# The left operands of a Strassen-like matmul kernel are placed at 32 different offsets in their ring tiles

## The chip, the cores and the metric

The kernel runs on one core of one Trainium2 chip, as one launch. The metric is device time in microseconds (us), from the first to the last instruction of the launch. Engines are named as in the profile: PE is the matmul engine, PEld its weight load, DVE the vector engine, ACT the activation engine, POOL the general-purpose engine, SP the engine that issues most DMAs. A matmul here has a left operand (128 columns, loaded into the array as weights, PEld) and a right operand (up to 512 columns, streamed through it).

## The reference

One decoder block on 1024 tokens of width 1024, in float32:

```python
def reference(x, mem, norm_mix, w_in, ...):
    h = x
    for i in range(DEPTH):                      # DEPTH = 1
        h = h + hybrid_mixer(rmsnorm(h, norm_mix[i]), w_in[i], ...)
        h = h + mem_cross_attention(rmsnorm(h, norm_xattn[i]), rmsnorm(mem, norm_mem[i]), ...)
        h = h + swiglu(rmsnorm(h, norm_ffn[i]), w_ffn_in[i], w_ffn_out[i])
    return rmsnorm(h, norm_final)
```

The mixer multiplies the normed input by `w_in` (1024 x 7712), runs two recurrent branches (an SSD scan with 16 heads and a gated linear attention with 4 heads) on slices of the product, multiplies each by a 1024 x 1024 matrix, gates and adds them, and multiplies by `w_o`. Cross-attention has four heads on 256 memory tokens. The feed-forward layer (FFN) is `(silu(n @ w_g) * (n @ w_u)) @ w_ffn_out` with 2816 hidden columns.

## The kernel before

**Arithmetic.** Activations are held transposed: 128 channels in the partitions, tokens along the row. Every large product is computed as three matmuls in the type fp32r: each operand is split into a high part (ACT copies it with rounding to fp32r) and a low part (DVE subtracts the high part from the source), and high x high, high x low and low x high are summed in PSUM. `split` (L226) is that pair of instructions.

**Units.** The products with `w_in` and with the two input matrices of the FFN use a seven-product (Strassen-like) scheme. A `Unit` takes 256 columns of the weight matrix and 1024 of its rows, as a raw tile of 8 KB per partition. `Operands` holds the seven combinations of the right operand (`B11`, `B21`, `T1`, `B22`, `T2`, `T3`, `T4`), each split into a high and a low tile, once for all units. For each of the seven products, `Unit.step` forms the left combination from the raw tile (some of these need an addition on DVE or POOL, into a tile named `sa`), takes one high and one low tile from a ring (`wring`, L230; names `whi` and `wlo`, three buffers of each, 640 fp32 wide), splits into them, and issues 12 matmuls: four blocks of 128 columns (`k`), three matmuls each, into one PSUM bank. `evac` then adds the bank into the unit's output, on DVE or ACT. The left operand of block `k` is `hi[:, k*128:(k+1)*128]`, that is 512 bytes per partition.

There are 48 units: 26 for `w_in`, made in the order conv inputs (6), `z` (4), `r` (4), `q` and `k` (4), the two gates (4 and 4), and 22 for the FFN, made later (a gate unit and an up unit for each of 11 column blocks). So 48 x 7 x 12 = 4032 matmuls read their left operand from the ring.

**Other users of the ring.** The memory's key and value products (`kv_unit`, L574) and the product that gives `v` (`v_steps`, L675) take ring tiles as well, and so does a prefetch of gates (`gate`, L1338). In `v_steps` the ring tile is the right operand: 264 columns per block, so its blocks start 0 and 1056 bytes into the tile.

**Other large products.** `dense` (names `hl`, `wd`) and the second FFN matrix (names `fs`) take their operands from other tiles ("slots" of 8 KB).

**Where tiles lie.** A ring tile is 640 x 4 = 2560 bytes per partition, which is 5 x 512, and a slot is 8192 bytes, 16 x 512. In the built program the ring tiles and all slots that hold operands of fp32r matmuls begin at 128 modulo 512, so in a unit the left operand lies a multiple of 512 bytes from the right one.

**Order.** The instruction order on each engine is made by the framework's scheduler from the program order and priorities; the splits and the evacuations of a unit are issued with a raised priority (`ahead`, 200 steps). In the SSD stage PE's order is the program's own.

Of the kernel before, what the change touches and what calls it, by code (L numbers as in the profile page):

```python
# [10 lines left out]
F32R = mybir.dt.float32r  # L11
# [5 lines left out]
P = 128  # L17
# [61 lines left out]
def block_kernel(ctx: ExitStack, tc: tile.TileContext, t: dict, out: bass.AP):  # L79
# [10 lines left out]
    def pool(name, bufs=1, space=None, stack=None):  # L90
        kw = {"reuse_waits": "tile"} if space is None else {"space": space}
        return (stack or ctx).enter_context(tc.tile_pool(name=name, bufs=bufs, **kw))
# [3 lines left out]
    wp = pool("w", 3)  # L96
# [25 lines left out]
    def acc():  # L122
        return ps.tile([P, 512], F32, name="acc", tag="acc", bufs=4)
# [56 lines left out]
    gcol, at = {}, 0  # L180
# [45 lines left out]
    def split(src, hi, lo, e=None):  # L226
        ACT.activation(hi, src, AF.Copy)  # L227
        sub(e or DVE, lo, src, hi)

    def wring():  # L230

        return [wp.tile([P, 640], F32R, name=n, tag=n, bufs=3)[:, :528] for n in ("whi", "wlo")]

    class Operands:

# [13 lines left out]
        def __init__(s, hb, kh, first=None, key="op", swap=0, last_key=None, order=None):  # L249
            s.B, s.kh, s.key, s.done, s.swap = {}, kh, key, 0, swap  # L250
            s.order = order or tuple(s.PLAN)
            s.last_key = last_key or key
            s.steps = s.build(hb, kh, first or (lambda *a: None))
# [25 lines left out]
    class Unit:  # L279
# [6 lines left out]
        def __init__(s, W, row0, c0, kh=4, post=None, key="aux", okey=None, side=None):  # L286
            s.W, s.row0, s.c0, s.kh, s.post, s.key, s.okey, s.side = W, row0, c0, kh, post, key, okey or key, side or key
            s.raw = s.S1 = s.S2 = s.e = None

        def load(s):  # L290
            if s.raw is None:
                s.raw = slot(s.key, (P, 2 * s.kh, 256), name="raw")
                SP.dma_start(s.raw, s.W[s.row0:s.row0 + 256 * s.kh, s.c0:s.c0 + 256].rearrange("(k p) c -> p k c", p=P))
# [30 lines left out]
        def step(s, name, B, cs=ALL, again=False):  # L324
            s.load()
            kh = s.kh
            if name == "B11":
                s.banks, s.swap, s.u = {}, B.swap, False
                s.out()
            if again:  # L330
                wh, wl = s.w
            else:
                with ahead():
                    src = s.left(name)
                    hi, lo = wring()
                    s.w = wh, wl = [x[:, :kh * P].rearrange("p (k c) -> p k c", c=P) for x in (hi, lo)]
                    split(src, wh, wl)
            xh, xl = B[name]
            key = s.BANK[name]
            fresh = key not in s.banks  # L340
            if fresh:
                s.banks[key] = acc()
            p = s.banks[key]
            m = 0
            for k in range(kh):
                for x, y in ((wh, xh), (wh, xl), (wl, xh)):
                    PE.matmul(p[:, cs], x[:, k, :], y[:, k, cs], start=fresh and m == 0, stop=m == 3 * kh - 1,
                              skip_group_check=True)
                    m += 1
            s.evac(name, p, cs)  # L350
# [213 lines left out]
    def kv_unit(c0):  # L564
# [7 lines left out]
        for kk in range(4):  # L572
            with ahead():
                hi, lo = wring()  # L574
                hv = hi[:, :512].rearrange("p (k c) -> p k c", c=256)
                lv = lo[:, :512].rearrange("p (k c) -> p k c", c=256)
                split(raw[:, 2 * kk:2 * kk + 2, :], hv, lv)
            for i in range(2):
                o = pa[i][:, :256]
                for k2 in range(2):  # L580
                    k = 2 * kk + k2
                    for m, (x, y) in enumerate(((hv, mh), (lv, mh), (hv, ml))):
                        w_, m_ = x[:, k2, :], y[:, k, :]
                        if c0 < D:
                            PE.matmul(o, w_[:, i * P:(i + 1) * P], m_, start=k == 0 and m == 0, stop=k == 7 and m == 2)
                        else:
                            PE.matmul(o, m_[:, i * P:(i + 1) * P], w_, start=k == 0 and m == 0, stop=k == 7 and m == 2)
            yield
# [60 lines left out]
    def v_steps():  # L649
        for pr in range(2):  # L650
# [12 lines left out]
            for n, name in enumerate(CHAIN):  # L663
                parts = []
                with ahead():
                    if name == "T1":
                        add(DVE, sa, A21, A22)
                    elif name == "B22":
                        sub(DVE, sa, sa, A11)
                        sub(DVE, A12, A12, sa)  # L670
                    elif name == "T2":
                        sub(DVE, A21, A11, A21)
                    a = (A11, A12, sa, A12, sa, A21, A22)[n]
                    for k2 in range(2):
                        hi, lo = wring()  # L675
                        hv, lv = hi.rearrange("p (k c) -> p k c", c=HW), lo.rearrange("p (k c) -> p k c", c=HW)
                        split(a[:, 2 * k2:2 * k2 + 2, :], hv, lv)
                        parts.append((hv, lv))
# [791 lines left out]
    at = [Att(h, j) for h in range(4) for j in (1, 0)]  # L1470
# [16 lines left out]


    rbc2 = u_xo_stats.sum
    gu = []  # L1490
    for u in range(D_FF // 256):
        def gpost(i, j, ap):
# [194 lines left out]
    for x, (n, k, kn) in enumerate(todo):  # L1687
        name = CHAIN[n]
# [62 lines left out]
```

## Time and profile before

| what | value |
|---|---|
| median of 2 timed runs | 1947.66 us (1947.66 to 1947.67) |
| span of the profiled execution | 1949.0 us |
| PE busy | 1916.2 us, 9776 instructions |
| PEld busy | 1615.6 us |
| DVE busy | 1298.5 us |
| ACT busy | 845.8 us |
| POOL busy | 557.8 us |
| mean granted TensorE clock | 0.998 |

The profiled execution took 1949.0 us from its first to its last instruction, 1.3 us more than the median of the timed runs. A matmul's record lasts longer than the distance from its start to the next one's, because matmuls overlap in the array and their ends are modelled: what a matmul costs is read from the distance between starts, or from the length of a piece of the chain of waits divided by the matmuls in it. The mean duration in the table of groups is not that cost.

### The profile page before, as it was taken

To read this page: it belongs to the slowest core of one execution; us is meant where nothing else is said; L and a number is where in the kernel's file an instruction comes from. 1 tells how busy PE (TensorE), PEld (TensorE's weight loads), DVE (VectorE), ACT (ScalarE), POOL (GpSimd) and SP (SyncE) were. 2 spreads that over 40 slices of the span, in tenths; PEclk is the share of its full clock that TensorE was granted. 3 is DMA by queue.
4 is the path that set the end of the run, shared out by engine and by line. 5 is a ranking of instruction groups with operands and counts; after the bars stand their busy time and mean duration, and the time that the engine had idled before them with its cause. 6 is when DMAs were issued, how large, how long until landed. Compare 5 with 4: busy or idle time off the path is not lost.

```text
span 1949.0 us, 26264 instructions
## 1 busy us (share of the span) xinstructions
PE 1916.2 (98%) x9776; PEld 1615.6 (83%) x9776; DVE 1298.5 (67%) x1873; ACT 845.8 (43%) x1485; POOL 557.8 (29%) x428
## 2 busy tenths in 40 slices
PE   7999999999999999999999999999999999999998
PEld 7998787888878888788887888888888888888888
DVE  7766879877776764655534237677777777766566
ACT  7534564655553444643223235444333333345243
POOL 0012334345543231022433000006445544320002
PEclk9999999999999999999999999999999999999999
DMA  9423383446553653997675201442233224177463
GB/s 341 144 93 101 130 307 107 152 161 186 174 173 123 198 167 124 348 346 270 226 269 164 82 22 44 140 141 82 90 126 110 82 100 144 42 271 239 157 224 126
DMA packets 237875, 317.98 MB, mean 163 GB/s; under 512 B 16538, under 2 KB 156036, under 8 KB 237748
## 3 DMA queue, kind: packets, MB, share of 16 engines
q1 hardware_dynamic: 236020, 310.01, 47.4%
q10 hardware_dynamic: 1728, 6.29, 0.8%
q8 instruction: 77, 1.26, 0.3%
q14 instruction: 50, 0.41, 0.1%
HBM read 215.27 MB, written 100.99 MB: 162 GB/s over the span
## 4 chain that ended last, share of the span: by engine, by line
PE 43%; DMA 3%; POOL 2%; DVE 1%; issue 1%; ACT 1%; POOLq 0%; SPq 0%; DVEq 0%; ACTq 0%
PE acc L51 38%; PE bank L51 4%; DMA pre<-in_w_ffn_out_dram 1%; POOL pre L73 1%; DMA down_d<-pre 1%; PE bank L55 1%; POOL ssum L73 0%; DVE hl L73 0%; POOL sa L73 0%; DMA h_d<-ga 0%; DMA ga<-vm_d 0%; DVE wd L73 0%; ACT wd L227 0%; ACT sq L493 0%; DVE phl L73 0%
## 5 line engine op out<-in xcount | busy, mean ns | idle before, releaser
L51 PE MATMUL acc<-hl,wd 128*128 128x512 f32 x1920 | 440.4, 390 | 3.6 <-DVE wd L73 2.0
L51 PEld LDWEIGHTS acc<-hl,wd 128*128 128x128 f32 x1920 | 359.6, 188 | 80.7 <-DVE wd L73 3.3
L73 DVE TENSOR_TENSOR wlo<-raw,whi 128x512 fp32r<-128x512 f32 x272 | 236.4, 875 | 103.6 <-ACT whi L227 103.5
L227 ACT ACTIVATE whi<-raw 128x512 fp32r<-128x512 f32 x272 | 169.5, 629 | 247.6 <-PE acc L51 201.0
L73 DVE TENSOR_TENSOR o<-acc,o 128x512 f32<-128x512 f32 (+1 forms) x256 | 172.6, 676 | 108.8 <-PE acc L51 95.4
L51 PE MATMUL acc<-fs 128*128 128x512 f32 (+1 forms) x792 | 155.7, 356 | 0.1
L51 PEld LDWEIGHTS acc<-fs 128*128 128x128 f32 x792 | 130.7, 189 | 20.8 <-issue 0.5
L73 DVE TENSOR_TENSOR fs<-fr,fs 128x1024 fp32r<-128x1024 f32 (+1 forms) x84 | 98.9, 1217 | 36.5 <-ACT fs L227 36.4
L227 ACT ACTIVATE fs<-fr 128x1024 fp32r<-128x1024 f32 (+1 forms) x84 | 79.2, 982 | 95.9 <-PE acc L51 31.2
L73 POOL TENSOR_TENSOR raw<-raw,sa 128x512 f32<-128x512 f32 x44 | 57.1, 1297 | 207.8 <-DVE wlo L73 207.8
L73 POOL TENSOR_TENSOR sa<-raw 128x512 f32<-128x512 f32 x43 | 69.6, 1619 | 107.0 <-DMA raw<-in_w_in_dram 78.9
L227 ACT ACTIVATE whi<-sa 128x512 fp32r<-128x512 f32 x96 | 59.6, 626 | 93.7 <-PE acc L51 92.3
L73 DVE TENSOR_TENSOR wlo<-sa,whi 128x512 fp32r<-128x512 f32 x96 | 80.9, 843 | 13.7 <-ACT whi L227 12.7
L73 DVE TENSOR_TENSOR wd<-raw,wd 128x1024 fp32r<-128x1024 f32 x40 | 52.8, 1323 | 47.6 <-ACT wd L227 47.2
L73 POOL TENSOR_TENSOR rstd<-rstd,mhalf 128x4 f32<-128x4 f32 (+1 forms) x7 | 8.7, 1246 | 257.0 <-DVE rstd L73 257.0
L227 ACT ACTIVATE wd<-raw 128x1024 fp32r<-128x1024 f32 x40 | 42.2, 1057 | 90.4 <-PE acc L51 89.8
L51 PE MATMUL acc<-T4h,whi 128*128 128x512 f32 x192 | 76.3, 397 | 2.4 <-DVE o L73 2.4
L51 PE MATMUL acc<-B22h,wlo 128*128 128x512 f32 x192 | 75.7, 394 | 1.5 <-DVE wlo L73 1.5
L51 PE MATMUL acc<-T1h,whi 128*128 128x512 f32 x192 | 76.3, 397 | 0.0
L51 PE MATMUL acc<-T2h,whi 128*128 128x512 f32 x192 | 75.9, 395 | 0.0
L51 PE MATMUL acc<-T3h,whi 128*128 128x512 f32 x192 | 75.9, 395 | 0.0
L51 PE MATMUL acc<-B22h,whi 128*128 128x512 f32 x192 | 75.7, 394 | 0.0
(399 smaller groups left out, 4698.6 us busy)
## 6 DMA issues: line engine op xcount, KB each, us to landing
raw<-in_w_in_dram SPq DMA_DIRECT2D x26, 1024.0 KB, 5.9
raw<-in_w_ffn_in_dram SPq DMA_DIRECT2D x22, 1024.0 KB, 6.5
act_d<-o SPq DMA_DIRECT2D x77, 256.0 KB, 2.1
fr<-act_d SPq DMA_DIRECT2D x35, 512.0 KB, 7.9
pre<-in_w_ffn_out_dram SPq DMA_DIRECT2D x11, 1024.0 KB, 10.0
fr<-down_d SPq DMA_DIRECT2D x20, 512.0 KB, 3.9
down_d<-pre SPq DMA_DIRECT2D x33, 256.0 KB, 3.1
h_d<-ga SPq DMA_DIRECT2D x32, 256.0 KB, 3.1
```

The costliest lines, as they stand in the source:

```text
L51: return s.e.matmul(o, x, y, **kw)
L55: return s.e.transpose(o, x, i)
L73: return f(*a, **kw)
L227: ACT.activation(hi, src, AF.Copy)
```

## The change

A unit now gets a number when it is made (`place`), and keeps `at = 4 * (number % 32)` elements, that is 16 bytes times the number modulo 32. `wring(at)` returns the slice of each ring tile that starts there. The counter starts at 22 for the `w_in` units (offsets 352 to 496 bytes, then 0 to 240) and is set to 0 before the FFN's units (0 to 336 bytes). The tiles' size (640) and count are as before, so no other tile moves; the largest offset is 124 elements and a unit uses 512, which fits in 640. The other users of the ring call `wring()` and stay at offset 0. No instruction is added or taken away; the addresses that the splits write and the weight loads read are what changes.

```diff
-    def wring():
-
-        return [wp.tile([P, 640], F32R, name=n, tag=n, bufs=3)[:, :528] for n in ("whi", "wlo")]
+    place = [22]
+
+    def wring(at=0):
+
+        return [wp.tile([P, 640], F32R, name=n, tag=n, bufs=3)[:, at:min(at + 528, 640)] for n in ("whi", "wlo")]
...
             s.raw = s.S1 = s.S2 = s.e = None
+            s.at = 4 * (place[0] % 32)
+            place[0] += 1
...
-                    hi, lo = wring()
+                    hi, lo = wring(s.at)
...
     rbc2 = u_xo_stats.sum
+    place[0] = 0
     gu = []
```

## The prediction

> **What bounds the kernel now.** I read the page first: its span, the engines' busy time and the granted clock.
>
> ```profile
> span 1949.0 us, 26264 instructions
> PE 1916.2 (98%) x9776; PEld 1615.6 (83%) x9776; DVE 1298.5 (67%) x1873; ACT 845.8 (43%) x1485; POOL 557.8 (29%) x428
> PEclk9999999999999999999999999999999999999999
> ```
>
> PE is busy nearly all the time at full clock. Busy matmuls overlap, so I went on to the chain of waits in order of time, which gives a piece's length and its number of matmuls. Its columns are start, length, what.
>
> ```profile
> 1220.35 85.00 PE acc L51 x375
> ...
> 1320.48 459.26 PE acc L51 x2026
> 1779.74 59.84 PE bank L51 x264
> ```
>
> The first piece lies in the dense products (85.00 / 375 = 226.7 ns each), the second is nearly the whole first half of the FFN, where the left operands come from the ring (459.26 / 2026 = 226.7 ns), the third belongs to the second FFN matrix (59.84 / 264 = 226.7 ns). In all three one matmul follows another with no break: the kernel runs at PE's own rate, and what a 512-wide fp32r matmul costs from start to start is 226.7 ns in every one of them. The timeline inside the second piece shows the same from one matmul to the next (columns: start, length, then engine, line, operation):
>
> ```profile
> 1449.78 0.39 PE L51 MATMUL acc<-B22h,whi 128*128 128x512 f32 x1
> ...
> 1453.18 0.39 PE L51 MATMUL acc<-T4l,whi 128*128 128x512 f32 x1
> ```
>
> Fifteen steps lie between these two starts: 3.40 / 15 = 226.7 ns.
>
> **The change part by part.** The groups by line show whose operands move.
>
> ```profile
> L51 PE MATMUL acc<-hl,wd 128*128 128x512 f32 x1920 | 440.4, 390 | 3.6 <-DVE wd L73 2.0 <-ACT wd L227 1.4 <-DVE hl L73 0.2
> ...
> L51 PE MATMUL acc<-T4h,whi 128*128 128x512 f32 x192 | 76.3, 397 | 2.4 <-DVE o L73 2.4
> ...
> L51 PE MATMUL acc<-T4l,whi 128*128 128x512 f32 x192 | 74.7, 389 | 0.0
> ```
>
> The 21 groups from the second row to the third (the seven products by three) read the ring; 21 x 192 = 4032 matmuls, or 4032 x 226.7 ns = 914 us, 47% of the span. The groups on `hl,wd` and `fs` keep their addresses. Of the 48 units two get offset 0 (the first made for the FFN, and the eleventh of `w_in`, whose number is 32), so 46 x 84 = 3864 matmuls get a distance other than 0 modulo 512. One nanosecond on each is 3.9 us, 0.2%. Two per cent of 1947.66 us, about what a measurement of this kernel can tell from no change, is 39 us or 10.1 ns on each. That one number decides the case.
>
> *The weight load.* It reads the same 512 bytes per block, from another start.
>
> ```profile
> L51 PEld LDWEIGHTS acc<-B11h,wlo x192: 187/188/192, 161.5 to 1703.0; 128*128 128x128 f32 x192
> ```
>
> It takes 188 ns under a matmul step of 226.7, so it has 39 ns of cover. If it grew by less, nothing should show; if that cover goes, the excess is paid on each of the 3864.
>
> *The matmul, with its operands at another distance.* No fp32r unit matmul of this kernel has it, so this is the unknown cost, to be bounded by the nearest rows. The nearest are the `v` products: there the ring tile is the right operand, and of its two blocks one lies 0 and one 1056 bytes, 32 modulo 512, from the left one.
>
> ```profile
> 127.75 0.28 PE L51 MATMUL acc<-whi,B21h 128*128 128x264 f32 x1
> ...
> 128.12 0.28 PE L51 MATMUL acc<-whi,B21h 128*128 128x264 f32 x1
> ...
> 128.48 0.28 PE L51 MATMUL acc<-whi,B21h 128*128 128x264 f32 x1
> ```
>
> In the program's order the three matmuls from the first row on read the block at 0 and the three from the second row the block at 32: 0.37 us against 0.36. With the starts rounded to 0.01 us, three matmuls at 32 bytes take 0.01 us less, give or take 0.02, so each costs between 10 ns less and 3 ns more than at 0. The next nearest are transposes in plain fp32, whose operands are `ident` and a source: in the built program the source `xt` lies at 0 from it and the source `xz` at 128 one way, 384 the other, modulo 512.
>
> ```profile
> 18.73 1.47 PE L55 MATMUL bank<-ident,xt 128*128 128x128 f32 x12
> ...
> 439.76 0.60 PE L55 MATMUL bank<-ident,xz 128*128 128x128 f32 x4
> ```
>
> One record lasts 0.27 us in the groups, so the steps are (1.47 - 0.27) / 11 = 0.109 us and (0.60 - 0.27) / 3 = 0.110 us. Again no difference, with a full weight load under each step. The single-transpose duration behind it:
>
> ```profile
> L55 PE MATMUL bank<-ident,xt 128*128 128x128 f32 x64 | 8.3, 272 | 0.0
> ```
>
> I take 0 ns as the value, from the `v` rows, because those are fp32r matmuls with the same kind of weight load. They cover one distance of 31 and the transposes another in another type, so the ends of the range stay wide; what could be at the other distances is priced under the rivals.
>
> *The splits.* ACT and DVE write the ring from another start. The rows are of the view by tile (minimum, median and maximum in ns), of a window (busy us of PE, PEld, DVE, ACT and POOL, then the clock and the DMA) and of PE's waits (total us, times, longest).
>
> ```profile
> L73 DVE TENSOR_TENSOR wlo<-raw,whi x272: 658/685/1789, 9.8 to 1713.8; 128x512 fp32r<-128x512 f32 x136
> L73 DVE SCALAR_TENSOR_TENSOR cv<-o,cols,cv x36: 1273/1279/2303, 264.5 to 372.3; 128x1021 f32<-128x1021 f32 x12, 128x1022 f32<-128x1022 f32 x12, 128x1023 f32<-128x1023 f32 x12
> 1400.00:1600.00 200.00, 200.00 (x884) 165.63 (x883) 153.54 (x190) 67.37 (x116) 96.13 (x64) 1.00 0.30 99
> PE acc L51 <- DVE wlo L73: 3.7, 7, 1.7
> ```
>
> The convolution's writes start 12, 8 and 4 bytes into a row, and the three forms together run from 1273 to a median of 1279 ns, so a shifted write costs DVE nothing that shows; I take 0. Were it not so: in the FFN's stage DVE is busy 153.5 us of 200 and ACT 67.4 while PE has no break, and in the whole kernel PE waits 3.7 us for `wlo` in the matmuls into `acc`. A tenth more on a 685 ns split is 0.07 us in the 2.72 us of a product's 12 matmuls, under that cover. With the cover gone, 336 splits of 0.07 us would be 23 us.
>
> *The rest.* No instruction, DMA, wait or tile size is changed, and the ring keeps three buffers, so no queue is reordered by the diff itself.
>
> The sum against the profiled execution is 1949.0 + 0 = 1949.0 us. That span is 1.3 us over the median of the timed runs, 1947.66, so the forecast for a timed run is 1948.
>
> **The rivals.** *Slower: left and right reads get in each other's way at other distances.* The mechanism would sit in every unit matmul, where the next block's weights are read while the right operand streams. A price: the 256-wide matmuls of the last product give the part of a step that doesn't grow with the width.
>
> ```profile
> 1927.70 3.96 PE acc L51 x33
> ```
>
> A 256-wide step is 3.96 / 33 = 120 ns; two of them less one 512-wide step leave 240 - 226.7 = 13.3 ns of fixed cost. If a clash doubled it, 3864 x 13.3 ns = 51 us would be added: 1999 us; at half of the distances, 1973. It is over 2% from 10.1 ns on each. For it: all large matmuls of this kernel run at one distance, 0, so the trace hardly says what the others cost. Against it: the `v` rows and the transposes.
>
> *Faster: the fixed cost is itself a clash at distance 0, and goes.* [...]
>
> ```profile
> 704.85 0.60 PE L51 MATMUL bank<-v,attm 128*128 128x256 f32 x2
> 705.29 0.59 PE L51 MATMUL bank<-sm,qk 128*128 128x256 f32 x2
> 705.72 0.59 PE L51 MATMUL bank<-v,attm 128*128 128x256 f32 x2
> ```
>
> Each step there is 0.87 / 4 = 217.5 ns, 9.2 under 226.7. If the shifted distances brought the unit matmuls down to that, 3864 x 9.2 ns = 36 us would go: 1912 us; if the whole 13.3 ns went, 1896. Against it: those fp32 operands also lie at 0 modulo 512, so the lower cost there needs no other distance, and the `v` rows keep their cost at 32.
>
> [...]
>
> *The change doesn't reach the time*, because another wait hides it in either direction. In the FFN's piece PE has no break, so this could only be in part; its time is the forecast's.
>
> **How the numbers follow.** The forecast has 0.57 (1943 to 1953 is its own range), and the last rival 0.03 at the same time. The slower rival has 0.30, as the trace has little to say on 30 of the 31 distances; I give 0.24 of it to more than 2% and 0.06 to less, since a clash at few distances or of few ns stays under. The faster one has 0.10, half of it over 2%, which needs more than the fp32 rows' 9.2 ns. So faster 0.05, within 2% 0.71, slower 0.24. The range goes up to 1999, the doubled fixed cost, leaving out about a tenth above it, and down to 1930, half of the faster rival's 36 us, leaving out less than a tenth.
>
> **What would show it.** If I am right, the long piece of the chain in the FFN still gives 226.7 ns a matmul, in each unit, and PEld stays at 188 ns. If the slower rival is right, the steps differ from unit to unit with the unit's offset while `hl,wd` and `fs` stay at 226.7. If the faster one is, they fall toward 217 in most units and not in the FFN's first. If the splits are to blame, PE's waits for `wlo` grow, DVE's 685 ns rises, and the steps inside a product stay.

## The result and the profile after

The changed kernel took 1962.1 us (median of 2 runs, 1960.4 to 1963.8) against 1947.7 us before: ratio 1.0075, 95% interval 1.0056 to 1.0094. It is 0.75% slower, about 14.5 us, inside the 2% that was called no change and clear of the measurement's own scatter. The profiled execution is the run timed at 1963.8 us; that its span, 1962.1 us, equals the median is a coincidence.

The page of the changed kernel:

```profile
span 1962.1 us, 26264 instructions
PE 1932.2 (98%) x9776; PEld 1615.1 (82%) x9776; DVE 1299.9 (66%) x1873; ACT 848.2 (43%) x1485; POOL 555.6 (28%) x428
PEclk9999999999999999999999999999999999999999
```

The instructions are as many as before and the clock is full (granted 0.999, before 0.998). The order of the instructions on PE, DVE, ACT and POOL is the same too. PE's busy time grew by 16.0 us, the other engines' by 2.4 us at most, and the weight loads' not at all. The chain of waits (start, length, what) tells where:

```profile
1091.46 77.08 PE acc L51 x370
1224.44 85.00 PE acc L51 x375
1324.61 468.26 PE acc L51 x2026
1792.86 59.84 PE bank L51 x264
```

The dense products and the second FFN matrix run as before (85.00 / 375 and 59.84 / 264 are both 226.7 ns a matmul). The FFN's long piece has the same 2026 matmuls and takes 468.26 us, where it took 459.26. 1761 of them read the ring, so that is 9.00 us / 1761 = 5.1 ns on each. The piece also starts 4.13 us later (1324.61 against 1320.48), and 4.13 + 9.00 = 13.13 us is the whole growth of the span (1962.1 - 1949.0). The 4.13 us come from the `w_in` units: by the starts in the trace their 2184 steps take 7.3 us more, and PE's steps outside the ring, waits included, 3.1 us less in sum.

The splits did not slow down, and PE does not wait more for them (by tile: minimum, median, maximum in ns; then PE's waits: total us, times, longest):

```profile
L73 DVE TENSOR_TENSOR wlo<-raw,whi x272: 657/685/1821, 9.7 to 1726.7; 128x512 fp32r<-128x512 f32 x136
L51 PEld LDWEIGHTS acc<-B11h,wlo x192: 187/188/192, 161.0 to 1715.6; 128*128 128x128 f32 x192
PE acc L51 <- DVE wlo L73: 3.5, 4, 1.7
```

Apart from some 3 us at its ends, where it overlaps its neighbours, each FFN unit from the third on has a stretch of its own, so the chain of waits in a window inside one unit gives that unit's rate. These are the rows for the units at 96, 176, 240, 256 and 272 bytes, in this order:

```profile
1421.88 16.16 PE acc L51 x69
...
1520.40 15.64 PE acc L51 x68
...
1598.97 14.16 PE acc L51 x62
...
1616.78 15.43 PE acc L51 x68
...
1635.83 15.19 PE acc L51 x67
```

That is 234.2, 230.0, 228.4, 226.9 and 226.7 ns a matmul. The same can be worked out for all 32 distances from the starts of PE's 512-wide fp32r matmuls (mean of the steps under 300 ns between two such matmuls, counted at the distance of the one that ends the step; distance of left from right in bytes, modulo 512; the entry at 0 holds the dense and the second FFN products too):

```
distance    0    16    32    48    64    80    96   112   128   144   160   176   192   208   224   240
step    227.0 230.5 233.2 233.2 233.2 232.0 234.0 233.2 232.9 232.3 233.4 230.0 229.4 232.3 233.1 228.4
distance  256   272   288   304   320   336   352   368   384   400   416   432   448   464   480   496
step    226.9 227.6 233.2 233.3 233.2 231.8 234.1 233.5 233.2 233.3 233.4 230.1 230.5 233.3 233.2 226.9
```

But for 16 and 240 bytes the two rows agree within 1.1 ns: the cost repeats every 256 bytes, not 512. It is nothing at 0, 0 to 4 ns within 16 bytes of it, and 2 to 7 ns elsewhere. No distance has a mean under 226.7 ns.

The entry at 16 is a mixture of two rates, and it shows that the distance is not the whole story. These are rows from the `w_in` unit at 16 bytes:

```profile
385.48 0.39 PE L51 MATMUL acc<-B11h,whi 128*128 128x512 f32 x1
...
388.20 0.39 PE L51 MATMUL acc<-T2h,whi 128*128 128x512 f32 x1
...
400.24 0.40 PE L51 MATMUL acc<-T3h,whi 128*128 128x512 f32 x1
...
403.04 0.40 PE L51 MATMUL acc<-B22h,whi 128*128 128x512 f32 x1
```

From the first row to the second 12 steps take 2.72 us, 226.7 ns each; from the third to the fourth 12 steps take 2.80 us, 233.3 ns each, at the same distance. The first 24 steps of the unit follow the unit at 0 without a break and average 226.7 ns. Then narrower matmuls of the SSD stage break the stream, and none of the 54 steps behind them (those under 300 ns) is under 232 ns.

A break shows at distance 0 as well. In the kernel before, the first three steps of a stretch of 512-wide fp32r matmuls (after other matmuls or a wait) average 232.7, 232.1 and 231.1 ns, and they fall to 226.7 by the tenth. So a step depends on the distance and on how the matmuls before it ran: at 0 a slow stream falls back to 226.7 ns, and at 16 it stayed as it was, fast or slow.

### The profile page after: what moved, and what is told of

It reads as the page before. It is cut to its first block, busy times and chain, and to the rows that moved or that the text cites. A ratio compares the mean times of both kernels' runs of the same rounds, so it can differ in the third digit from the quotient of the medians.

```text
span 1962.1 us, 26264 instructions
## 1 busy us (share of the span) xinstructions
PE 1932.2 (98%) x9776; PEld 1615.1 (82%) x9776; DVE 1299.9 (66%) x1873; ACT 848.2 (43%) x1485; POOL 555.6 (28%) x428
## 4 chain that ended last, share of the span: by engine, by line
PE 44%; DMA 3%; POOL 2%; issue 1%; DVE 1%; ACT 0%; SPq 0%; POOLq 0%; DVEq 0%; ACTq 0%
PE acc L51 39%; PE bank L51 4%; DMA pre<-in_w_ffn_out_dram 1%; POOL pre L73 1%; DMA down_d<-pre 1%; DMA h_d<-ga 1%; PE bank L55 1%; POOL ssum L73 0%; POOL sa L73 0%; DVE phl L73 0%; DMA ga<-kT_d 0%; DVE hl L73 0%; DVE pe L73 0%; ACT sq L497 0%; DVE wd L73 0%
```

## The experiments

All of them change the kernel before. Theory D says that the distance between the starts of the left and the right operand, modulo 256, sets the step. Its rivals: the absolute start of the left operand (A), a period of 512 (P512), the change of offsets as such, a cost of the splits, or something particular to the ring or the units.

**Both operands moved together.**

```diff
     dr = pool("dram", 1, bass.MemoryType.DRAM)
+    pad = pool("pad").tile([P, 24], F32, name="pad")
     wp = pool("w", 3)
```

> A 96-byte tile in front of the ring moves the ring and all slots together: every left and right operand of an fp32r matmul starts 96 bytes later (at 224 modulo 512), the distance stays 0. Theory D (the distance between left and right decides): steps of 512 columns stay at 226.7 ns in the unit matmuls, hl,wd and fs alike, time 1948 us, ratio 1.000. Theory A (the start of the left operand alone decides, as the units of the changed kernel whose left operand starts at 224 took about 234 ns a step): all 6744 steps of 512 columns gain about 7 ns, 47 us, time about 1995 us, ratio 1.024.

Measured: 1947.9 us, ratio 1.0002 (0.9992 to 1.0011). In the chain of waits:

```profile
1219.19 85.00 PE acc L51 x375
1319.33 459.26 PE acc L51 x2026
```

The left operands start at 224 modulo 512, as those of the changed kernel's slowest units did, and a step takes 226.7 ns. Theory A falls.

**The right operand alone moved.**

```diff
     wp = pool("w", 3)
+    pad = pool("pad").tile([P, 24], F32, name="pad")
```

> The 96-byte tile lies between the ring and the slots: left operands of the units stay where they were before (128 modulo 512), the right ones move to 224, so all 4032 unit matmuls have the distance 416 (160 modulo 256); hl,wd and fs move as pairs and keep 0. Theory D: about 233.4 ns a step in the units (from the changed kernel's unit matmuls at 160 and 416), 4032 x 6.7 = 27 us, of which some is taken back by waits elsewhere: 1970 to 1975 us, ratio 1.012 to 1.014; hl,wd and fs at 226.7. Theory A: units at 226.7 ns, 1948 us, ratio 1.000.

Measured: 1965.8 us, ratio 1.0095 (1.0079 to 1.0112).

```profile
1226.71 85.25 PE acc L51 x375
1327.30 471.06 PE acc L51 x2026
```

With the left operands where they always were, the FFN's piece grows by 11.80 us, 6.7 ns on each of 1761 unit matmuls, as D says. The total is 4 us under what was expected: the ring's steps with a wait among them got shorter, so waits took back more than I allowed (6.4 us in the `w_in` stage, by the starts in the trace).

**A fixed 256 bytes.**

```diff
-        return [wp.tile([P, 640], F32R, name=n, tag=n, bufs=3)[:, :528] for n in ("whi", "wlo")]
+        return [wp.tile([P, 640], F32R, name=n, tag=n, bufs=3)[:, a:min(a + 528, 640)]
+                for n, a in zip(("whi", "wlo"), ats)]
...
-                    hi, lo = wring()
+                    hi, lo = wring((64, 64))
```

> All 48 units write and read their ring tiles 256 bytes further on. Theory P256 (the cost repeats every 256 bytes of distance, as in the changed kernel, where the unit at 256 took 226.9 ns a step): 226.7 ns, 1948 us, ratio 1.000. Theory P512 (it repeats every 512 bytes, and only 0 is free): about 232 ns, 4032 x 5 = 20 us, 1965 to 1968 us, ratio 1.010. A cost of splits that write elsewhere than at the tile's start would show here as well, as more waiting of the matmul engine for wlo.

Measured: 1947.6 us, ratio 1.000 (0.999 to 1.001).

```profile
1318.12 459.26 PE acc L51 x2026
```

The step is 226.7 ns at 256 bytes. P512 falls, and so does a cost of splits that write further on in the tile.

**A fixed 96 bytes**, by the same edit with `wring((24, 24))`.

> All 48 units lie 96 bytes further on in their ring tiles, the distance at which the changed kernel's units were slowest (234.0 ns a step, 7.3 over before). Theory D: 4032 x 7.3 = 29 us more in the unit matmuls, of which waits elsewhere take some back: 1972 to 1977 us, ratio 1.013 to 1.015. Rival: the cost comes from changing the offset from unit to unit (two offsets in flight at once), not from the offset: 1948 us, ratio 1.000.

Measured: 1968.7 us, ratio 1.0112 (1.0097 to 1.0127).

```profile
1223.24 85.27 PE acc L51 x375
1323.90 472.66 PE acc L51 x2026
```

13.40 us / 1761 = 7.6 ns on each unit matmul, with one offset for all units. A change of offset from unit to unit isn't needed. The total is again under the expected one, by 3 us, for the same reason. Here a stretch does not recover after a break: its first 20 steps stay between 232 and 237 ns by their place, where those of the kernel before are at 226.7 from the tenth on.

**The low parts alone at 96 bytes**, with `wring((0, 24))`.

> Only the low parts (wlo) of the units lie 96 bytes further on; the high parts stay at 0. Of the three matmuls of a block (high x right-high, high x right-low, low x right-high) the low part is read as weights while the second one streams, and is itself in the array while the third streams. Theory N (the load of the next weights meets the right operand that is streaming): the step from the start of the second matmul to the start of the third takes about 234 ns, the other two 226.7. Theory O (a matmul pays for its own two operands): the step after the start of the third takes 234 ns, the other two 226.7. Either way 1344 x 7.3 = 10 us, 1956 to 1958 us, ratio 1.004 to 1.005; if hi and lo parts together were needed, 1.000.

Measured: 1961.4 us, ratio 1.0062 (1.0045 to 1.0079), more than either theory allowed. In the timeline of the FFN:

```profile
1501.40 0.39 PE L51 MATMUL acc<-T2h,whi 128*128 128x512 f32 x1
...
1503.50 0.39 PE L51 MATMUL acc<-T2h,whi 128*128 128x512 f32 x1
```

Nine steps, three blocks, take 2.10 us: 233 ns each on average, though two of three matmuls have distance 0. Over all units the three steps of a block are 233.1 ns (after high x right-high), 231.6 (after high x right-low) and 232.5 (after low x right-high). Both N and O fall as they were put: every step is slow, and one shifted low part costs some 17 ns a block, more than twice the 7.6 ns of a shifted matmul among shifted ones.

**The low parts at 256 bytes**, with `wring((0, 64))`, to see whether the jump between two offsets is what costs.

> High parts at 0, low parts 256 bytes further on. Seen before: with the low parts at 96 all three steps of a block were slow (233.1, 231.6, 232.5 ns), the two between distances of 0 as well. Theory D (each operand's distance counts modulo 256, and a disturbed load also delays the next few): all distances are 0 modulo 256, so 226.7 ns a step, 1948 us, ratio 1.000. Theory J (a jump of the left operand's offset from one load to the next costs, whatever the distance): steps near 232 ns, 4032 x 5 = 20 us less what waits take back, 1961 us, ratio 1.006.

Measured: 1947.3 us, ratio 1.000 (0.999 to 1.001).

```profile
1317.27 459.26 PE acc L51 x2026
```

A jump by 256 bytes from load to load is free (459.26 / 2026 = 226.7 ns a step). It is the distance of the low parts that slows the high parts' steps.

**The low parts at 96 bytes, and last in each product.**

```diff
-            for k in range(kh):
-                for x, y in ((wh, xh), (wh, xl), (wl, xh)):
-                    PE.matmul(p[:, cs], x[:, k, :], y[:, k, cs], ...)
-                    m += 1
+            for pairs in (((wh, xh), (wh, xl)), ((wl, xh),)):
+                for k in range(kh):
+                    for x, y in pairs:
+                        PE.matmul(p[:, cs], x[:, k, :], y[:, k, cs], ...)
+                        m += 1
...
-                    hi, lo = wring()
+                    hi, lo = wring((0, 24))
```

> Low parts at 96, and the 12 matmuls of a product in another order: the eight with high parts first, then the four with low parts. Theory D with an after-effect (a load at 96 clashes, and the next loads at 0 need some steps to fall back): the four low steps about 234 ns, the first one to three high steps after them 231 to 233, the rest 226.7; 336 x (4 x 7.3 + 2 x 6) = 14 us at most, 1958 to 1962 us, ratio 1.005 to 1.007. Theory M (a product pays at every step when its two parts have different offsets): all 12 steps near 232 ns, 20 us, ratio 1.007 to 1.010.

Measured: 1952.1 us, ratio 1.0023 (1.0012 to 1.0033), under what either theory said. Eight high matmuls and four low ones in the timeline:

```profile
1500.55 0.39 PE L51 MATMUL acc<-T3h,whi 128*128 128x512 f32 x1
...
1502.36 1.09 PE L51 MATMUL acc<-T3h,wlo 128*128 128x512 f32 x4
1503.30 0.39 PE L51 MATMUL acc<-B22h,whi 128*128 128x512 f32 x1
```

The eight steps from the first row to the second take 1.81 us, 226 ns each; the four from the second to the third 0.94 us, 235 ns each. Over all units the high steps are 227.0 to 228.3 ns by their place and the low ones 230.9 to 237.1. Theory M falls: the high parts run freely once they are together. The after-effect that I had added to D is near nothing here (1 ns on the first four high steps, not 5), so an after-effect of one to three steps behind every shifted low part is not what slowed the high steps in the run with alternating parts.

**The same order at offset 0** (the loop of the last diff alone).

> The order of the experiment with the low parts last, at offset 0: the order alone. Every theory: 226.7 ns a step and 1948 us within 3 us, as each load still reads 512 bytes under a matmul step.

Measured: 1945.8 us in one run, within the scatter of the kernel before beside it (1945.1 to 1950.8).

```profile
1316.92 457.90 PE acc L51 x2020
```

457.90 / 2020 is 226.7 ns: the order is free. Against it the piece of the run before took 462.34 us for as many matmuls, 587 of them with a low part at 96: 4.44 us / 587 = 7.6 ns on each, and nothing on the others.

**Other matmuls: the dense products.**

```diff
+    pad = pool("pad", stack=st5).tile([P, 24], F32, name="pad")
     open_slots("m", 4, st5)
```

> Ring and units as before. A 96-byte tile is put before the slots that hold wd, the left operands of the five dense 1024-wide products, so that these 1920 matmuls have the distance 96. Theory D, if it holds for any pair of operands: 234 ns a step in hl,wd, 1920 x 7.3 = 14 us, 1958 to 1962 us, and units at 226.7. If the cost belongs to the ring's tiles or to the Strassen-like units: 226.7 ns in hl,wd, 1948 us.

Measured: 1959.7 us in one run, 11.6 us over the median of the kernel before on the same chip.

```profile
1091.13 79.36 PE acc L51 x370
1226.91 87.60 PE acc L51 x375
1329.56 459.26 PE acc L51 x2026
```

Now the dense pieces pay: 79.36 and 87.60 us, where the kernel before has 77.08 and 85.00. The second is 87.60 / 375 = 233.6 ns a matmul, and the units are at 226.7. The cost belongs neither to the ring nor to the units; these 512-wide fp32r pairs pay it as well. (In the built program the tile also moves operands of 72 other matmuls of 512 columns and of 240 of 256 columns.)

**The ring without padding.**

```diff
-        return [wp.tile([P, 640], F32R, name=n, tag=n, bufs=3)[:, :528] for n in ("whi", "wlo")]
+        return [wp.tile([P, 528], F32R, name=n, tag=n, bufs=3)[:, :528] for n in ("whi", "wlo")]
```

> The ring tiles are 528 fp32 wide (2112 bytes, 4 x 512 + 64) in place of 640, so the three high buffers lie 128, 192 and 256 bytes from the right operands and the three low ones 320, 384 and 448, all modulo 512. By the steps of the changed kernel's units at these distances (233, 229, 227 and 233, 233, 230) the mean step is 230.6, 3.9 over before: 4032 x 3.9 = 16 us, of which waits take some back: 1960 to 1964 us, ratio 1.006 to 1.008. If the distance didn't decide: 1948 us.

Measured: 1956.5 us, ratio 1.0041 (1.0026 to 1.0056), a little less than expected.

```profile
1320.50 466.44 PE acc L51 x2026
```

The FFN's piece gives 7.18 us / 1761 = 4.1 ns on each unit matmul, near the 3.9 from the table of distances. That the mean came out is partly luck: by distance the steps are 230.1 ns at 256, where 227 was expected, and 230.7 at 128, where 233 was. Among matmuls at other distances a matmul doesn't pay what its own distance costs in a stream of its kind. So the 448 unused bytes of each ring tile are worth 0.4% here.

**The narrow products moved by 96 bytes**: `wring((24, 24))` in the key, value and `v` products, the units as before.

> Units as before. The ring tiles of the key, value and v products lie 96 bytes further on: 264-wide matmuls at the distances 416 and 384, 256-wide ones at 96 and 416. Theory W (a narrow step is set by its weight load, which is why the v products of the kernel before showed nothing at 32 bytes): steps of 264 columns stay at 121 to 122 ns, those of 256 at 120. Rival (every step pays about 7 ns at these distances, and 32 bytes on the right side was a free one): 128 ns and 127 ns, 672 x 7 + 384 x 7 = 7 us in the first 180 us.

Measured: 1950.2 us in one run, which says nothing by itself. The timeline of the `v` products:

```profile
127.81 0.29 PE L51 MATMUL acc<-whi,B21l 128*128 128x264 f32 x1
...
130.92 0.29 PE L51 MATMUL acc<-wlo,B21h 128*128 128x264 f32 x1
```

From the first row to the last 25 steps take 3.11 us, 124.4 ns each. The same products in the kernel before take 3.15 us for 26 steps (127.75 to 130.90), 121.2 ns each. Matmuls at 416 and at 384 take turns in small groups, so which of the two pays can't be told: counted at the matmul that begins the step, the median is 126 ns at 416 and 123 at 384; counted at the one that ends it, 124 and 125. The kernel before has 121 to 122 at 0 and 480 either way. The medians of the 256-wide steps lie between 118 and 121 ns at 0, 96 and 416. In the run with the right operands moved, the 264-wide products lay at 64 and 96 bytes, and their medians stayed at 121 to 122 ns. Both expectations miss: 264-wide matmuls paid some 3 ns here, about half of what wide ones pay, and nothing at 64, 96 and 480 bytes, where wide ones pay 6 to 7 ns.

## Why the prediction was right or wrong

The forecast was no change, 1948 us, and the likeliest case did not come: 1962.1 us lies outside the forecast's own 1943 to 1953. It lies in the wide range and within 2% of before because the slower rival came in a mild form, a case that had a chance of 0.06. So the agreement is luck as far as the mechanism of the forecast goes. The 2% taken for what a measurement can tell was also too coarse: the runs of the kernel before lie between 1945 and 1953 us, and the intervals of the ratios here are 0.1 to 0.2% to either side.

- *What bounds the kernel*: right. PE's own step sets the time; 5.1 ns more on each of 1761 matmuls came out as 9.00 us of span.
- *The count*: right. The operands that keep their addresses (`hl,wd`, `fs`) stayed at 226.7 ns, and the growth is in the units.
- *The weight load* stays at 188 ns, as forecast; that duration does not show the cost, so its cover of 39 ns was the wrong thing to look at.
- *The matmul with its operands at another distance, 0 ns from the `v` rows*: this is the step that failed. 14.5 us / 3864 is 3.8 ns on each matmul in the total, and 2 to 7 ns in the steps themselves at most distances. The `v` rows were one width (264) and one distance (480), and at that very distance a 512-wide step takes 233.2 ns. The transposes, the second row, are in plain fp32, whose steps (0.109 us at 0, 0.110 at 128 bytes) show no difference where the 512-wide fp32r steps of the changed kernel pay 6 ns (232.9 against 226.7). They are also 128 columns wide. "Nearest row" was taken by the kind of instruction and not by its width and type.
- *The slower rival*: that the step depends on the distance of the two operands is what the runs show (that it is their reads that clash is inferred), and its sign for it, steps that differ from unit to unit with `hl,wd` and `fs` unchanged, is what the trace shows. Its price, a doubled fixed cost of 13.3 ns on each, was too large: the worst distance costs 7.6 ns, and the mean over the 3864 in the total is 3.8. Of the 7.3 us that the steps of the `w_in` units gained, shorter steps elsewhere took back 3.1.
- *The faster rival*: wrong. No distance brings the mean step under 226.7 ns, so the fixed cost is not a clash at distance 0. Its 9.2 ns and 36 us compare a 256-wide record in plain fp32 (217.5 ns) with a 512-wide fp32r step; no run shows that the two do the same work. In its place the runs showed 226.7 ns or more at each of the 32 distances.
- *The splits and the rest*: right. `wlo` takes 685 ns as before, waits for it did not grow, and a shift by 256 bytes is free.

What stays open is which two reads meet, or whether it is reads that meet at all. The low parts at 96 cost 7.6 ns each when they follow one another, with nearly nothing on the high parts, and some 17 ns a block when they alternate with high parts, spread over all three steps. That is neither a load of the next weights that meets the running stream, nor a matmul paying for its own two operands, as the two theories were put. That a step also depends on the steps before it (the unit at 16, the stretches after a break) may be why the order matters, but no run separates this. The period of 256 bytes and the cheap places next to 0 and 256 are measured, not explained.

## What to carry to other kernels

For 512-wide fp32r matmuls on a kernel bound by PE, try a placement in which the starts of the left and right operands are equal modulo 256 bytes: here the step was then 226.7 ns, and 2 to 7 ns more at most other distances. Ring tiles of 2560 bytes, ten times 256, kept it in this kernel; tiles of 2112 bytes, with 448 bytes less of padding, cost 0.4%. Moving both operands together by 96 bytes changed nothing (226.7 ns a step). Even at distance 0 a break in the stream made the next nine or so steps longer, some 29 ns a stretch in the kernel before, which no run here tried to save. Check it by the step from start to start, piece by piece of the chain of waits; the durations of the weight loads (188 ns before and after) don't show it. When a cost is bounded from rows that lie far off, take rows of the same width and type; if there are none, treat it as unknown.

## What the runs showed of the hardware

In an unbroken stream a 512-wide fp32r matmul step is 226.7 ns when the starts of its operands are equal modulo 256 bytes, and 228 to 234 ns at distances more than 16 bytes from that (and at 240), whichever operand is moved (left at 96: 7.6 ns more on each; right moved so that the distance is 416: 6.7; both together: 0). At distance 0 the first steps after a break take 231 to 233 ns and reach 226.7 by the tenth; at 96 they don't recover; at 16 a stream stayed fast (226.7) or slow (233.4) as it had been. A shifted part among unshifted ones slows the unshifted ones as well when they alternate (233 ns on average), and hardly when they are grouped (226 against 235 ns).
